# A hybrid decoder step on one core: loads, transposes and page loads of the S5 stage in another order

## The chip, the cores and the metric

The kernel runs on one NeuronCore of one Trainium2 chip. The metric is the device time of one execution in microseconds (us). The time before is the median of three runs.

## What is computed

One inference step of a small decoder: 256 prompt tokens and 8 sample tokens pass through one S5 layer (a complex diagonal state-space mixer) with its MLP and one sparse-attention layer with its MLP. The change touches the first stage of the program, in which two independent things are computed. One is the S5 mixer up to its gelu:

```python
bbar_r = zoh_r[..., None] * br - zoh_i[..., None] * bi
bu_r = jnp.einsum('btgc,gpc->btgp', u, bbar_r)
acr, aci, bcr, bci = lax.associative_scan(_complex_affine_combine, (a_r, a_i, bu_r, bu_i), axis=1)
sr = bcr + acr * s0r - aci * s0i
y = einsum(c_re, sr) - einsum(c_im, si)
z = jax.nn.gelu(y + d_skip * h) @ w_glu
```

The other depends on no token of this step: the compression of the paged cache, which the attention layer needs much later.

```python
past_cmp = cache_cmp_kv[page_table].reshape((nb, past_len) + row_shape)
blk = rows.reshape(nb, n_blk, CMP_BLOCK, 2, N_KV_HEADS, HEAD_DIM) + cmp_pos
hid = jax.nn.gelu(jnp.einsum('bnlsgd,sldh->bnsgh', blk, w1))
```

## The kernel before, in words

Activations lie feature by token: 8 tiles of 128 features by 264 tokens (`NT`). After the first stage come the gated projection `glu` (16 weight tiles), an MLP (64 weight tiles), keys and values, attention, the output projection and a second MLP. A weight tile is 512 KB; ACT splits it into a rounded part `wh` (L609), DVE into the rest `wl` (L610), and TensorE (PE) does three products of each part (L616 to L618). Four tiles of the pool `wr` hold raw weights, and the compression's weights `w` share these four.

The first stage, `s5_stage`, is written in the order in which it is to be issued (`manual_schedule`), and each engine takes its instructions in that order. Its steps, for the two halves h = 0 and 1 of the state slots:

- DVE makes the powers of the transition (`PT`, up to L270) and `e` (L325 to L328); ACT turns the last powers into `pr`, `pq`, `CQ` (`as_mult(PT, 3, 5, True)`, L257 to L306); DVE makes `E[h]` from them (`powers_in`, L332 to L335).
- PE sums the squares of the tokens (L309), DVE makes the norm's `rB` (L496 to L137) and scales the tokens `U` (L503); PE broadcasts `rB` (L510).
- `transpose_in(h)`: PE transposes `E[h]` (L349, 16 each), ACT copies it out (L351). `chunk_in(h)`: PE multiplies it with the tokens (L367, 64 each), ACT copies into the states `St`.
- DVE: `xhat` (L524), the powers on the output side `Fc[0]`, `Fc[1]` (`powers_out`, L383 to L386), the scan over chunks (`up` and `carry`, L443 to L446, then `down`, L465 and L466: slots 0 to 15, 16 to 23, 24 to 31). `Fc[0]` takes the buffer that `E[1]` leaves.
- PE: the convolution kernels (`kernels(h)`, L409 to L413), the convolutions (`conv`, L473) of eight feature tiles `ft`, and `from_states(ft)` (L482), which needs the scanned states of the tile's four slots. ACT: the gelu `ge` (L485, two buffers) and its rounded copy `gh` (L486). DVE: the rest `gl = ge - gh` (`rests`, L548), which frees `ge`.

Between these steps `filler(n)` advances the generator `sample_compress` by n pieces. For each of s = 0 (keys) and 1 (values) it runs 32 matmuls of 272 columns (L809; one instruction of the order is two matmul records of the trace), four groups `lc` of 8, two pieces a group. A page block `blk` has one buffer: 16 pages, one DMA each at a page number read from the table (128 KB, L788), and the position row (L789). So the block of s = 1 is loaded when the last matmul of s = 0 has read the block of s = 0. The counts are in a table:

```python
F = dict(m=2, n=4, o=3, q=4, r=5)
    K.load_cst()
    filler(1)
    as_mult(PT, 3, 5, True)
...
    filler(F["m"])
    gain(0)
    powers_in(0)
```

m stands ahead of `powers_in(0)`, n behind `chunk_in(0)`, o ahead of `powers_out`, q between `kernels(0)` and `kernels(1)`, r behind the first six convolutions. `load_cst` (L1501) and the two loads of `comp_loads` (L733, L736) are issued by ACT; all other loads of the stage but four early ones by the sync engine SP. SP reads the 16 page numbers by `value_load` with bounds (L781): a load from SBUF, an operation on the register and an assertion each. At the end of the stage DVE does:

```python
    for s0, n, late in ((0, 16, ()), (16, 8, (0, 1, 2, 3)), (24, 8, (4, 5))):
        down(s0, n)
        rests(late)
```

A transfer's completion is counted on one of eight semaphores (DMAHW0 to DMAHW7 in the order below). They go round, and a transfer waits, in its issuer's queue, for the earlier one on its semaphore.

Of the kernel before, what the change touches and what calls it, by code (L numbers as in the profile page):

```python
# [153 lines left out]

F = dict(m=2, n=4, o=3, q=4, r=5)


def s5_stage(K, filler):
# [141 lines left out]
    for h in range(2):  # L300
        S.activation(sq[:, h], U[:, h], AF.Square)
    K.load_cst()
    filler(1)
    as_mult(PT, 3, 5, True)
# [132 lines left out]
    def step(dst, src, n, i):  # L437

        sh = [128, 2, 32, n]
        a = tp.tile([128, 2, 32, 8], F32, tag="va", name="ca", bufs=1)[:, :, :, 0:n]  # L440
        b_ = tp.tile([128, 2, 32, 8], F32, tag="vb", name="cb", bufs=1)[:, :, :, 0:n]
        x, o = St[:, :, :, src:src + n], St[:, :, :, dst:dst + n]
        TT(a, x, SX[:, i, 1:2].to_broadcast([128, 2, 32]).unsqueeze(3).to_broadcast(sh), ALU.mult)  # L443
        TT(b_, x[:, ::-1], SX[:, i, 0:3:2].unsqueeze(3).to_broadcast(sh), ALU.mult)
        TT(o, o, a, ALU.add)
        TT(o, o, b_, ALU.add)  # L446
# [42 lines left out]

    filler(F["m"])  # L490
    gain(0)
# [54 lines left out]
    def rests(fts):  # L546
        for ft in fts:
            TT(yl[0][:, ft], ges[ft], yh[0][:, ft].bitcast(F32), ALU.subtract)  # L548
    for s0, n, late in ((0, 16, ()), (16, 8, (0, 1, 2, 3)), (24, 8, (4, 5))):
        down(s0, n)  # L550
        rests(late)
        for ft in range(s0 // 4, (s0 + n) // 4):
            ges[ft] = from_states(ft, pys[ft])
            if ft in (1, 3):
                expand(1, 4 * ft - 4, 8)
    K.last_scan = [i for i in nc.cur_bb.bb.instructions if i.engine == nc.vector.engine][-1]
    rests((6, 7))
# [171 lines left out]
def comp_loads(K):  # L729
    nc = K.nc  # L730
    c = K.cp
    K.w2 = c.tile([128, 4, 64], F32, name="w2")
    nc.scalar.dma_start(K.w2, K.A["cmp_w2"].rearrange("(x p) e -> p x e", p=128))  # L733

    K.gk = c.tile([128, 4, 64], F32, name="gk")
    nc.scalar.dma_start(K.gk.rearrange("p a d -> p (a d)"), K.A["gains"].broadcast_to((128, 256)))  # L736

# [39 lines left out]
def sample_compress(K):  # L777

    nc = K.nc
    S, V, G = nc.scalar, nc.vector, nc.gpsimd  # L780
    K.pages = [nc.sync.value_load(K.ptab[0:1, i:i + 1], min_val=0, max_val=NPOOL - 1) for i in range(16)]  # L781
    w1v = K.A["cmp_w1"]

    def load(s):
        blk = K.fil.tile([128, 17, 16, 16], F32, tag="blk", name="blk")
        f = lambda t: t.rearrange("p l x -> p (l x)")
        for pg in range(16):
            nc.sync.dma_start(f(blk[:, pg]), K.A["cache_cmp"][s, bass.ds(K.pages[pg], 1)].rearrange("o p x -> (o p) x"))  # L788
        nc.sync.dma_start(f(blk[:, 16]), K.A["cmp_pos"][s])  # L789
        return blk  # L790
# [5 lines left out]
    w = {(0, lc): load_w(0, lc) for lc in range(2)}  # L796
    blk = load(0)
    yield
    for lc in (2, 3):
        w[0, lc] = load_w(0, lc)  # L800
    comp_loads(K)
    yield
    for s in range(2):
        pts = [K.ps("fl"), K.ps("fl")]
        for lc in range(4):
            for l in range(4):
                for hf in range(2):
                    ll = 4 * lc + l
                    nc.tensor.matmul(pts[hf][:, 0:272], w[s, lc][:, l, 128 * hf:128 * hf + 128], blk[:, :, ll],  # L809
                                     start=(ll == 0), stop=(ll == 15))  # L810
                if l == 1:
                    yield
            if s == 0:
                w[1, lc] = load_w(1, lc)
            if s == 0 and lc == 3:
                blk = load(1)
            yield
        if s == 0:
            comp_setup(K)
# [648 lines left out]
def build(ctx, tc, A, O):  # L1468
# [31 lines left out]
    K.wr = ctx.enter_context(tc.tile_pool(name="wr", bufs=4))  # L1500
    K.load_cst = lambda: nc.scalar.dma_start(ctile, A["cst"])  # L1501

# [184 lines left out]
def inputs_of(x):  # L1687

    cat = np.concatenate
    cmp = x["cache_cmp_kv"].reshape(20, 4, 2, 8, 2, 2, 4, 64).transpose(5, 0, 4, 7, 2, 3, 1, 6).reshape(2, 20, 128, 256)  # L1690
    pos = x["cmp_pos"].reshape(2, 16, 128).transpose(0, 2, 1)
    slc, win = x["cache_slc_kv"], x["cache_win_kv"]
# [73 lines left out]
```

## Time and profile before

| | before |
|---|---|
| median of 3 runs | 757.06 us (756.28 to 759.0) |
| profiled execution, own time | 756.5 us |
| its span, first to last instruction | 754.7 us |
| mean granted TensorE clock | 0.948 |
| busy, share of the span | PE 94%, DVE 70%, ACT 54%, POOL 8% |
| DMA | 124.67 MB, mean 165 GB/s |

Times of rows are microseconds from the span's start. PE, PEld (weight loads), DVE, ACT, POOL are engines, SPq and ACTq the sequencers that issue DMAs; L12 is a line of the kernel. Text in brackets at the end of a row is the idle time of the engine just before it and what ended it. A wait for several things is put down to the one that came last.

### The profile page before, as it was taken

What the parts mean: (1) busy time and instruction counts of PE and PEld (TensorE: products, weight loads), DVE (VectorE), ACT (ScalarE), POOL (GpSimd) and SP (SyncE); (2) the same over time, 40 slices, a digit from 0 to 9 for tenths busy, and PEclk for the clock granted to TensorE, in tenths of its full rate; (3) what the DMA queues carried; (4) which work ended last, traced back from release to release, by engine and by line L of the source; (5) the groups of instructions that cost most, each with busy time, mean ns of one, the idle gap of its engine ahead of it and who ended that gap; (6) DMA issues with size and microseconds to landing.
All of it is one profiled execution on the core that took longest, in us unless ns stands there. A gap on an engine that the chain in (4) does not pass through costs nothing.

```text
span 754.7 us, 16057 instructions
## 1 busy us (share of the span) xinstructions
PE 709.4 (94%) x6160; PEld 644.4 (85%) x6160; DVE 525.7 (70%) x1154; ACT 404.9 (54%) x918; POOL 58.3 (8%) x103
## 2 busy tenths in 40 slices
PE   3495989999999999999989999999999999999998
PEld 1384879999999999999978956455799999999997
DVE  7679977988767756655776787746387777755553
ACT  4257246656666645444574666434376666644442
POOL 0100000210400000001022231100020000000000
PEclk9697999999999999999999968667999999999999
DMA  6714115665997655555546551000155555566651
GB/s 254 257 63 147 58 57 163 210 203 184 334 377 266 217 186 178 186 179 184 181 146 217 181 184 57 1 1 1 56 167 170 188 176 187 177 194 192 196 189 43
DMA packets 48430, 124.67 MB, mean 165 GB/s; under 512 B 5978, under 2 KB 21978, under 8 KB 48098
## 3 DMA queue, kind: packets, MB, share of 16 engines
q1 hardware_dynamic: 46818, 121.23, 48.8%
q10 hardware_dynamic: 1536, 2.42, 0.9%
q8 instruction: 48, 0.79, 0.4%
q14 instruction: 28, 0.23, 0.1%
HBM read 120.63 MB, written 7.18 MB: 169 GB/s over the span
## 4 chain that ended last, share of the span: by engine, by line
PE 87%; DVE 3%; SPq 3%; DMA 3%; ACT 2%; issue 2%; ACTq 0%; DVEq 0%
PE ps_mm L616 22%; PE ps_mm L617 21%; PE ps_mm L618 21%; PE ps_fl L809 5%; PE ps_sc L1213 3%; PE ps_tr L1250 2%; SPq L788 2%; PE ps_po L1271 2%; DMA raw<-w_up_in 1%; SPq L781 1%; PE ps_mm L1424 1%; PE ps_sc L1216 1%; DVE wl L610 1%; DMA xp<-x_cols_in 1%; PE ps_sc L1209 1%
## 5 line engine op out<-in xcount | busy, mean ns | idle before, releaser
L610 DVE TENSOR_TENSOR wl<-raw,wh 128x512 fp32r<-128x512 f32 x344 | 241.0, 705 | 145.4 <-ACT wh L609 143.1
L609 ACT ACTIVATE wh<-raw 128x512 fp32r<-128x512 f32 x344 | 215.3, 630 | 208.2 <-PE ps_mm L617 150.9
L616 PE MATMUL ps_mm<-hh,wh 128*128 128x264 f32 x512 | 145.2, 284 | 0.0
L617 PE MATMUL ps_mm<-hl,wh 128*128 128x264 f32 x512 | 145.0, 283 | 0.0
L618 PE MATMUL ps_mm<-hh,wl 128*128 128x264 f32 x512 | 145.0, 283 | 0.0
L617 PEld LDWEIGHTS ps_mm<-hl,wh 128*128 128x128 f32 x512 | 96.5, 188 | 0.0
L616 PEld LDWEIGHTS ps_mm<-hh,wh 128*128 128x128 f32 x512 | 96.4, 188 | 0.0
L618 PEld LDWEIGHTS ps_mm<-hh,wl 128*128 128x128 f32 x512 | 96.0, 187 | 0.0
L616 PE MATMUL ps_mm<-xhxl,wh 128*128 128x264 f32 x256 | 72.9, 285 | 0.0
L617 PE MATMUL ps_mm<-yl,wh 128*128 128x264 f32 x256 | 72.9, 285 | 0.0
L617 PE MATMUL ps_mm<-xhxl,wh 128*128 128x264 f32 x256 | 72.8, 285 | 0.0
L616 PE MATMUL ps_mm<-yh,wh 128*128 128x264 f32 x256 | 72.6, 284 | 0.0
L618 PE MATMUL ps_mm<-xhxl,wl 128*128 128x264 f32 x256 | 72.4, 284 | 0.2 <-DVE wl L610 0.2
L618 PE MATMUL ps_mm<-yh,wl 128*128 128x264 f32 x256 | 72.6, 284 | 0.0
L809 PE MATMUL ps_fl<-blk,w 128*128 128x272 f32 x128 | 35.6, 443 | 17.1 <-DMA xp<-x_cols_in 10.4
L618 PEld LDWEIGHTS ps_mm<-xhxl,wl 128*128 128x128 f32 x256 | 48.0, 188 | 0.4 <-DVE wl L610 0.4
L616 PEld LDWEIGHTS ps_mm<-xhxl,wh 128*128 128x128 f32 x256 | 48.2, 188 | 0.1
L616 PEld LDWEIGHTS ps_mm<-yh,wh 128*128 128x128 f32 x256 | 48.2, 188 | 0.0
L618 PEld LDWEIGHTS ps_mm<-yh,wl 128*128 128x128 f32 x256 | 48.2, 188 | 0.0
L617 PEld LDWEIGHTS ps_mm<-xhxl,wh 128*128 128x128 f32 x256 | 48.1, 188 | 0.0
L617 PEld LDWEIGHTS ps_mm<-yl,wh 128*128 128x128 f32 x256 | 48.1, 188 | 0.0
L809 PEld LDWEIGHTS ps_fl<-blk,w 128*128 128x128 f32 x128 | 27.3, 217 | 24.0 <-issue 10.8
(438 smaller groups left out, 1452.3 us busy)
## 6 DMA issues: line engine op xcount, KB each, us to landing
raw<-w_up_in SPq DMA_DIRECT2D x64, 512.0 KB, 4.3
raw<-w_down_in SPq DMA_DIRECT2D x64, 512.0 KB, 3.6
raw<-s_w_glu_in SPq DMA_DIRECT2D x16, 512.0 KB, 4.3
w<-cmp_w_in SPq DMA_DIRECT2D x12, 512.0 KB, 3.5
raw<-w_kv_in SPq DMA_DIRECT2D x12, 512.0 KB, 3.7
blk<-cache_cmp_in SPq DMA_DIRECT2D x32, 128.0 KB, 3.2
raw<-w_q_in SPq DMA_DIRECT2D x8, 512.0 KB, 4.1
win_old_out<-cache_win_kv_in SPq DMA_DIRECT2D x8, 510.0 KB, 6.3
```

Of the source, the lines that this page charges most:

```text
L609: nc.scalar.activation(h[:, :, cols], src[:, c:c + 4], AF.Copy)
L610: nc.vector.tensor_tensor(l[:, :, cols], src[:, c:c + 4], h[:, :, cols].bitcast(F32), ALU.subtract)
L616: nc.tensor.matmul(out, wh, xh, start=start, stop=False)
L617: nc.tensor.matmul(out, wh, xl, start=False, stop=False)
L618: nc.tensor.matmul(out, wl, xh, start=False, stop=stop)
L781: K.pages = [nc.sync.value_load(K.ptab[0:1, i:i + 1], min_val=0, max_val=NPOOL - 1) for i in range(16)]
L788: nc.sync.dma_start(f(blk[:, pg]), K.A["cache_cmp"][s, bass.ds(K.pages[pg], 1)].rearrange("o p x -> (o p) x"))
L809: nc.tensor.matmul(pts[hf][:, 0:272], w[s, lc][:, l, 128 * hf:128 * hf + 128], blk[:, :, ll], start=(ll == 0), stop=(ll == 15))
L1209: nc.tensor.matmul(banks[g2][:, 256 * r2:256 * r2 + 256], K.QT[hs[g2], 4 * gp + 2 * rp + r2, 0:128], K.KTp[hs[g2], gp, :, 0:128], start=Fa ...
L1213: nc.tensor.matmul(banks[g2], K.QT[hs[g2], 4 * gp + 2 * rp + u - 1, 128:256], K.KTp[hs[g2], gp], start=True, stop=False)
L1250: nc.tensor.transpose(pt[:, 128 * j:128 * j + 128], Pf[:, 128 * j:128 * j + 128], K.ident)
L1271: nc.tensor.matmul(po[64 * g2:64 * g2 + 64, 128 * kt:256], K.Vp[:, kt, br, 64 * g:64 * g + 64], rhs, start=False, stop=(br == 1 and kt == 1))
```

## The change

1. `load_cst` and the two loads of `comp_loads` are issued by SP, and `load_cst` stands earlier in the text.
2. The count m is gone, n keeps 4 and o becomes 5: no compression stands ahead of `powers_in(0)` and `transpose_in(0)`. Two pieces of the generator that only load are taken right behind the load of `xp`.
3. The block of pages is cut into halves of 8 rows each: 64 KB for a page, three buffers instead of one, 34 more DMAs. The tensors in HBM are laid out accordingly.
4. Page numbers are read without bounds.
5. The scan's products `ca` and `cb` lie in one `big` buffer of the pool instead of two small ones.
6. The rests of tiles 2 and 3 stand behind the last `down`, and the point behind which `glu` may be issued (`last_scan`) is that `down`.

```diff
-F = dict(m=2, n=4, o=3, q=4, r=5)
+F = dict(n=4, o=5, q=4, r=5)
     filler(1)
     xp = K.xp = e8([128, 8, NT], "xp")
     nc.sync.dma_start(xp, A["x_cols"])
+    filler(1)
+    K.load_cst()
+    filler(1)
...
-    K.load_cst()
-    filler(1)
     as_mult(PT, 3, 5, True)
...
-        a = tp.tile([128, 2, 32, 8], F32, tag="va", name="ca", bufs=1)[:, :, :, 0:n]
-        b_ = tp.tile([128, 2, 32, 8], F32, tag="vb", name="cb", bufs=1)[:, :, :, 0:n]
+        w = tp.tile([128, 2048], F32, tag="big", name="big")
+        a, b_ = (w[:, 512 * i:512 * i + 512].rearrange(...)[:, :, :, 0:n] for i in range(2))
...
-    filler(F["m"])
     gain(0)
...
-    for s0, n, late in ((0, 16, ()), (16, 8, (0, 1, 2, 3)), (24, 8, (4, 5))):
+    for s0, n, late in ((0, 16, ()), (16, 8, (0, 1)), (24, 8, (2, 3, 4, 5))):
         down(s0, n)
+        if s0 == 24:
+            K.last_scan = [i for i in nc.cur_bb.bb.instructions if i.engine == nc.vector.engine][-1]
         rests(late)
...
-    nc.scalar.dma_start(K.w2, ...)
+    nc.sync.dma_start(K.w2, ...)
-    nc.scalar.dma_start(K.gk.rearrange("p a d -> p (a d)"), ...)
+    nc.sync.dma_start(K.gk.rearrange("p a d -> p (a d)"), ...)
...
-    K.pages = [nc.sync.value_load(K.ptab[0:1, i:i + 1], min_val=0, max_val=NPOOL - 1) for i in range(16)]
+    K.pages = [nc.sync.value_load(K.ptab[0:1, i:i + 1]) for i in range(16)]
-    def load(s):
-        blk = K.fil.tile([128, 17, 16, 16], F32, tag="blk", name="blk")
+    def load(s, hf):
+        blk = K.fil.tile([128, 17, 8, 16], F32, tag="blk", name="blk", bufs=3)
...
-    blk = load(0)
+    blk = {(0, 0): load(0, 0)}
     yield
+    blk[0, 1] = load(0, 1)
     for lc in (2, 3):
         w[0, lc] = load_w(0, lc)
+    yield
     comp_loads(K)
+    blk[1, 0] = load(1, 0)
     yield
...
-            if s == 0 and lc == 3:
-                blk = load(1)
+            if s == 0 and lc == 1:
+                blk[1, 1] = load(1, 1)
...
-    K.load_cst = lambda: nc.scalar.dma_start(ctile, A["cst"])
+    K.load_cst = lambda: nc.sync.dma_start(ctile, A["cst"])
```

ACT's queue at the start of the stage, before (`sq`: squares of the tokens, `cst`, `w_389`, `gk`: the three late loads, `pr`, `pq`: the powers for `E`):

```order
L301 ACTIVATE sq<-U 128x1168 [waits DMAHW5_49]
L301 ACTIVATE sq<-U 128x1168 [waits DMAHW6_49]
L1501 DMA cst<-cst_in 128x1141 [waits DMAHW5_49]
L733 DMA w_389<-cmp_w_in 128x4x64 [waits DMAHW7_49]
L736 DMA gk<-gains_in 128x256 [waits DMAHW1_49]
L257 ACTIVATE pr<-px 128x128 [waits DVE_49]
L258 ACTIVATE pq<-px 128x4x16
```

and now:

```order
L304 ACTIVATE sq<-U 128x1168 [waits DMAHW5_49]
L304 ACTIVATE sq<-U 128x1168 [waits DMAHW6_49]
L260 ACTIVATE pr<-px 128x128 [waits DVE_49]
L261 ACTIVATE pq<-px 128x4x16
L262 ACTIVATE pq<-px 128x4x16
L307 ACTIVATE CQ<-pq 128x192 [waits Activation_49]
L330 ACTIVATE E_332<-e_333 128x32x16 [waits DVE_49]
```

The three DMAs with their waits have left ACT's queue; `pr` waits for DVE alone.

PE's queue at the same place, before (`sq,vec`: the sum of squares, `blk,w_261`: the first compression group, `ident,E_420`: the transposes of `E[0]`, `rB,vec`: the norm's broadcast):

```order
L309 MATMUL ps_tr<-sq,vec 128x511 x4
L309 MATMUL ps_tr<-sq,vec 128x292
L809 MATMUL ps_fl<-blk,w_261 128x272 x8
L349 MATMUL ps_tr<-ident,E_420 128x128 x16
L510 MATMUL ps_tr<-rB,vec 128x56
```

and now:

```order
L310 MATMUL ps_tr<-sq,vec 128x511 x4
L310 MATMUL ps_tr<-sq,vec 128x292
L350 MATMUL ps_tr<-ident,E_332 128x128 x16
L510 MATMUL ps_tr<-rB,vec 128x56
L510 MATMUL ps_tr<-rB,vec 128x7
```

The first group of the compression is gone from there. Behind `chunk_in(0)` two groups still stand ahead of the transposes of `E[1]`, as before, and two groups instead of one stand between `chunk_in(1)` and `kernels(0)`.

DVE's queue at the end of the stage, from the last two instructions of the last `down` on, before (`gl`: rests, `wl`: rests of the first weight tiles of `glu`, `z`: its first result):

```order
L465 TENSOR_TENSOR big<-St,sx 128x392
L466 TENSOR_TENSOR St<-St,big 128x8x7x7
L548 TENSOR_TENSOR gl<-ge,gh 128x264 x2
L610 TENSOR_TENSOR wl<-raw,wh 128x512 x4
L548 TENSOR_TENSOR gl<-ge,gh 128x264 x2
L610 TENSOR_TENSOR wl<-raw,wh 128x512 x3
L674 TENSOR_TENSOR z<-ps_mm,sg 128x264
```

and now:

```order
L466 TENSOR_TENSOR big<-St,sx 128x392
L467 TENSOR_TENSOR St<-St,big 128x8x7x7
L548 TENSOR_TENSOR gl<-ge,gh 128x264
L611 TENSOR_TENSOR wl<-raw,wh 128x512 x4
L548 TENSOR_TENSOR gl<-ge,gh 128x264 x5
L611 TENSOR_TENSOR wl<-raw,wh 128x512 x3
L675 TENSOR_TENSOR z<-ps_mm,sg 128x264
```

Of the four rests that stood ahead of the last `down`, two have moved behind it, and one of the later ones now stands ahead of the first weight tiles instead of two.

## Rows read from the trace of the kernel before

**Rows 1.** The page: busy us, share of the span and instructions of each engine.

```profile
PE 709.4 (94%) x6160; PEld 644.4 (85%) x6160; DVE 525.7 (70%) x1154; ACT 404.9 (54%) x918; POOL 58.3 (8%) x103
```

**Rows 2.** Waits, 0 to 125 us: engine, line <- releaser: us, times, longest.

```profile
ACT pr L257 <- DMA blk<-cache_cmp_in: 13.5, 1, 13.5
...
PE ps_fl L809 <- DMA blk<-cmp_pos_in: 6.7, 1, 6.7
```

**Rows 3.** Timeline, ACT's wait and DVE's: start, us, engine, line, operation.

```profile
15.89 0.69 DVE L328 TENSOR_TENSOR e<-e,big 128x512 f32<-128x512 f32 x1
...
22.24 0.36 ACTq L1501 DMA_DIRECT2D cst<-cst_in  x1
...
25.04 0.31 ACT L257 ACTIVATE pr<-px 128x128 f32<-128x128 f32 x1 [13.52 <-DMA blk<-cache_cmp_in]
...
25.38 1.76 DVE L332 TENSOR_TENSOR E<-e,pr 128x1536 f32<-128x1536 f32 x1 [8.80 <-ACT pr L257]
```

**Rows 4.** Timeline, from the norm to `powers_out(0)`.

```profile
11.07 7.22 PE L309 MATMUL ps_tr<-sq,vec 128*128 128x511 f32 x10 [11.07 <-DMA vec<-vecs_in]
...
28.84 1.76 DVE L335 TENSOR_TENSOR E<-E,big 128x1536 f32<-128x1536 f32 x1
...
34.74 0.36 DVE L137 SCALAR_TENSOR_TENSOR rB<-rs,rs 128x73 f32<-128x73 f32 x1
...
45.35 2.35 DVE L524 TENSOR_TENSOR xhat<-xp,rb 128x2112 f32<-128x2112 f32 x1
...
51.63 2.29 DVE L383 TENSOR_TENSOR Fc<-Cl,pr 128x2048 f32<-128x2048 f32 x1 [3.92 <-ACT ET L351]
```

**Rows 5.** The chain that ended last, PE's pieces, 0 to 125 us: start, us.

```profile
28.65 6.70 PE ps_fl L809 x16
...
37.13 2.67 PE ps_tr L510 x24
...
42.22 7.53 PE ps_fl L809 x32
49.75 1.78 PE ps_tr L349 x16
...
70.67 9.85 PE ps_fl L809 x32
...
102.08 2.63 PE ps_fl L473 x16
...
116.43 1.95 PE ps_fl L482 x120
```

**Rows 6.** Windows: stretch, busy us of PE, PEld, DVE, ACT, POOL, granted clock, DMA.

```profile
28.00:32.00 4.00, 3.35 (x8) 2.57 (x9) 3.93 (x5) 0.00 (x0) 0.00 (x0) 0.50 0.98 366
```

**Rows 7.** Timeline of DVE, the scan's end and what follows.

```profile
99.69 0.98 DVE L466 TENSOR_TENSOR St<-St,big 128x784 f32<-128x784 f32 x1
...
104.90 0.57 DVE L466 TENSOR_TENSOR St<-St,big 128x392 f32<-128x392 f32 x1
...
111.26 0.43 DVE L548 TENSOR_TENSOR gl<-ge,gh 128x264 fp32r<-128x264 f32 x1 [0.30 <-ACT gh L486]
...
115.81 0.57 DVE L466 TENSOR_TENSOR St<-St,big 128x392 f32<-128x392 f32 x1
...
116.98 2.49 DVE L610 TENSOR_TENSOR wl<-raw,wh 128x512 fp32r<-128x512 f32 x4
```

**Rows 8.** SP: page numbers and page loads (durations in ns min/median/max).

```profile
L781 SPq TENSOR_LOAD <-ptab x16: 263/263/469, 3.3 to 12.0; - x16
...
13.59 8.59 SPq L788 DMA_DIRECT2D blk<-cache_cmp_in  x16
...
L788 SPq DMA_DIRECT2D blk<-cache_cmp_in x32: 332/333/1281, 13.6 to 67.1; - x32
```

**Rows 9.** Timeline, gelu on ACT and the first products of `glu` on PE.

```profile
117.50 0.39 ACT L485 ACTIVATE ge<-ps_fl 128x264 f32<-128x264 f32 x1 [2.53 <-PE ps_fl L482]
...
123.88 0.29 PE L617 MATMUL ps_mm<-gl,wh 128*128 128x264 f32 x1
```

More of the change, by code (lines that the diff above doesn't have):

```diff
@@ L439, in step @@
         sh = [128, 2, 32, n]
-        a = tp.tile([128, 2, 32, 8], F32, tag="va", name="ca", bufs=1)[:, :, :, 0:n]
-        b_ = tp.tile([128, 2, 32, 8], F32, tag="vb", name="cb", bufs=1)[:, :, :, 0:n]
+        w = tp.tile([128, 2048], F32, tag="big", name="big")
+        a, b_ = (w[:, 512 * i:512 * i + 512].rearrange("p (r s n) -> p r s n", r=2, n=8)[:, :, :, 0:n] for i in range(2))
         x, o = St[:, :, :, src:src + n], St[:, :, :, dst:dst + n]
@@ L555, in s5_stage @@
                 expand(1, 4 * ft - 4, 8)
-    K.last_scan = [i for i in nc.cur_bb.bb.instructions if i.engine == nc.vector.engine][-1]
     rests((6, 7))
@@ L732, in comp_loads @@
     K.w2 = c.tile([128, 4, 64], F32, name="w2")
-    nc.scalar.dma_start(K.w2, K.A["cmp_w2"].rearrange("(x p) e -> p x e", p=128))
+    nc.sync.dma_start(K.w2, K.A["cmp_w2"].rearrange("(x p) e -> p x e", p=128))
     K.gk = c.tile([128, 4, 64], F32, name="gk")
-    nc.scalar.dma_start(K.gk.rearrange("p a d -> p (a d)"), K.A["gains"].broadcast_to((128, 256)))
+    nc.sync.dma_start(K.gk.rearrange("p a d -> p (a d)"), K.A["gains"].broadcast_to((128, 256)))
 def comp_setup(K):
@@ L780, in sample_compress @@
     S, V, G = nc.scalar, nc.vector, nc.gpsimd
-    K.pages = [nc.sync.value_load(K.ptab[0:1, i:i + 1], min_val=0, max_val=NPOOL - 1) for i in range(16)]
+    K.pages = [nc.sync.value_load(K.ptab[0:1, i:i + 1]) for i in range(16)]
     w1v = K.A["cmp_w1"]
-    def load(s):
-        blk = K.fil.tile([128, 17, 16, 16], F32, tag="blk", name="blk")
+    def load(s, hf):
+        blk = K.fil.tile([128, 17, 8, 16], F32, tag="blk", name="blk", bufs=3)
         f = lambda t: t.rearrange("p l x -> p (l x)")
         for pg in range(16):
-            nc.sync.dma_start(f(blk[:, pg]), K.A["cache_cmp"][s, bass.ds(K.pages[pg], 1)].rearrange("o p x -> (o p) x"))
-        nc.sync.dma_start(f(blk[:, 16]), K.A["cmp_pos"][s])
+            nc.sync.dma_start(f(blk[:, pg]), K.A["cache_cmp"][s, hf, bass.ds(K.pages[pg], 1)].rearrange("o p x -> (o p) x"))
+        nc.sync.dma_start(f(blk[:, 16]), K.A["cmp_pos"][s, hf])
         return blk
@@ L808, in sample_compress @@
                     ll = 4 * lc + l
-                    nc.tensor.matmul(pts[hf][:, 0:272], w[s, lc][:, l, 128 * hf:128 * hf + 128], blk[:, :, ll],
+                    nc.tensor.matmul(pts[hf][:, 0:272], w[s, lc][:, l, 128 * hf:128 * hf + 128], blk[s, lc // 2][:, :, ll % 8],
                                      start=(ll == 0), stop=(ll == 15))
@@ L1689, in inputs_of @@
     cat = np.concatenate
-    cmp = x["cache_cmp_kv"].reshape(20, 4, 2, 8, 2, 2, 4, 64).transpose(5, 0, 4, 7, 2, 3, 1, 6).reshape(2, 20, 128, 256)
-    pos = x["cmp_pos"].reshape(2, 16, 128).transpose(0, 2, 1)
+    cmp = x["cache_cmp_kv"].reshape(20, 4, 2, 8, 2, 2, 4, 64).transpose(5, 2, 0, 4, 7, 3, 1, 6).reshape(2, 2, 20, 128, 128)
+    pos = x["cmp_pos"].reshape(2, 2, 8, 128).transpose(0, 1, 3, 2)
     slc, win = x["cache_slc_kv"], x["cache_win_kv"]
@@ L1726, in inputs_of @@
         w_kv=tiles(x["w_kv"])[:, 0], w_q=wq, w_gate=w_in[:, 1024:1072].reshape(8, 128, 48).transpose(1, 0, 2), nsa_w_o=wo,
-        cmp_pos=np.repeat(pos[..., None], 16, -1).reshape(2, 128, 256),
+        cmp_pos=np.repeat(pos[..., None], 16, -1).reshape(2, 2, 128, 128),
         cmp_w1=x["cmp_w1"].reshape(2, 16, 128, 256).transpose(0, 2, 1, 3),
```

## The prediction, as put on record

> **What bounds the kernel now.** I began with the page: PE is busy 94% of the span, DVE 70% [rows 1]. That is an average. From about 118 us on PE streams products with small gaps, so the rest of the program moves with the moment at which `glu` can start, and nothing in the change edits what comes after. Only the first stage decides. There the waits name two large ones on engines that others wait for: ACT stands 13.5 us before `pr`, PE 6.7 us before a page block [rows 2].
>
> The timeline shows who pays for the first. DVE has finished `e` at 15.89 + 0.69 = 16.58 and sits idle until 25.38, 8.80 us, for `pr`; ACT starts `pr` at 25.04, right behind the DMA issues that began with `cst` at 22.24 [rows 3]. `pr` itself needs only DVE's powers, done before `e`. It is late because it is queued behind three DMAs which each wait for an older transfer on their semaphore (the order of ACT above), here page loads still in flight.
>
> Behind that, DVE runs without a gap to the end of `xhat` at 47.70, then waits 3.92 us for the buffer of `E[1]`, which PE's transposes leave at 51.63 [rows 4]. PE was late there: two compression groups, 7.53 us, stand ahead of the transposes [rows 5]. From 51.63 DVE has work without a gap to 104.90 + 0.57 = 105.47. Then the four rests ahead of the last `down` wait for gelus, and it ends only at 115.81 + 0.57 = 116.38 [rows 7]. PE brought the last convolutions at 104.71 [rows 5], so these gelus came late. So the stage is a chain DVE, PE, DVE, PE with three holes: 8.8, 3.9 and about 6 us.
>
> **Late loads on SP.** ACT reaches `pr` as soon as DVE's powers are there, before DVE needs it. `E` then starts at 16.58: 8.80 us earlier. The two ends are 8.80, where SP takes the waits, and 0, the second rival. I take 8.80: the row names a DMA as releaser and the DMA is no longer in ACT's queue.
>
> The row says that ACT's queue was blocked for 13.5 us [rows 2]. The Trainium skill (DMA: Bandwidth & Descriptors, Issuing engines are not separate DMA queues) says that all issuers share the same DMA engines and that spreading issues over several saves only the short time of issuing. By that, leaving ACT frees only three issues of about 0.36 us, 1.1 us in place of 8.8.
>
> On SP the three are issued behind the first two page halves. What waits behind them is the third half, needed by PE only near 57 us, so they cost nothing there.
>
> **Transposes ahead of the compression.** `E[0]` is ready at 28.84 + 1.76 = 30.60, now 21.80; `rB` at 35.10, now 26.30 [rows 4]. The sum of squares on PE ends at 18.3 [rows 4], so it is in time. The first compression group no longer blocks PE from 28.65 to 35.35 [rows 5], and the transposes fit between 21.8 and 26.3. From the broadcast to the start of the two groups behind `chunk_in(0)` PE took 42.22 - 37.13 = 5.1 us, the groups 7.53, and `Fc[0]` started 1.88 behind the transposes' start [rows 4, 5]. So `Fc[0]` starts at 26.3 + 5.1 + 7.5 + 1.9 = 40.8 if PE runs at its full clock. It will not quite: PE will have idled since 18.3, and the first group of before ran at a granted clock of 0.50, 1.2 GHz of 2.4 [rows 6], taking 6.70 us where half of 7.53 is 3.8: 2.9 us more [rows 5]. The ends are 0 and 2.9. I take 1.1, nearer to 0, because transposes and broadcast now run ahead of the compression and take some of the slow time in short instructions: 41.9. Below 38.9 it cannot go, since `xhat` ends there. Against 51.63 that is 9.7 us.
>
> **Three halves, three buffers.** The group moved behind `chunk_in(1)` makes PE's way to the last convolution longer by half of 7.53, 3.8 us. Its old way from the transposes' end (51.53) to that convolution (104.71) is 53.2 us [rows 5]. The 6.7 us for pages [rows 2] go, since the third half has a buffer of its own and is loaded early, and so do the 2.3 us by which the two groups behind that wait were slower than 7.53 (9.85, [rows 5]). 53.2 - 6.7 - 2.3 + 3.8 = 48.0, so PE is ready at about 89.8. DVE finishes the first `down` 49.0 us behind the start of `Fc[0]` (99.69 + 0.98 - 51.63, [rows 4, 7]), at 90.9. PE is 1 us ahead, and the first two rests have 3 us more, since they stand behind the second `down`. The cover is thin: if it goes, the first rival begins.
>
> SP pays for the halves: page issues come every 8.59/16 = 0.54 us [rows 8], so 34 more take 18 us. They start earlier, since the range checks go: one number took 0.56 us from load to load, of which the load is 0.26 [rows 8], so 16 save 4 to 5 us and the first half is issued by about 18 us and landed by 22. PE asks for it at 31. The second is issued by 28 and needed at 44, the third by 39 and needed at 57. The fourth follows the freed buffer at about 39, ends near 49 and is needed near 78. The weights `w` follow the freed buffers as before. So the checks alone bring nothing, and the halves cost nothing in the sum; the cover is at least 9 us everywhere.
>
> Of the page loads the rows show one every 0.54 us [rows 8]. The Trainium skill (DMA: Bandwidth & Descriptors, Rules for kernel authors) advises to coalesce small transfers, as under 64 KB one pays mostly overhead; a half page is just 64 KB. By that rule the halves speak against the change, which is the third rival.
>
> **One `big` buffer** for the scan's products: the order shows the same waits on DVE alone. Nothing.
>
> **The end.** From `Fc[0]` DVE needs 53.84 us to the second `down`'s end, two rests of 0.43, and 4.7 us for the last `down` (from about 111.7 to 116.38) [rows 4, 7]: 59.4 us, so it ends at 101.3 in place of 116.38, 15.1 us earlier. Something is given back. Rests 3 to 7 now stand behind four `wl` of `glu`, 2.49 us [rows 7], and a gelu waits until the rest of two tiles before has freed its buffer. Counted from the last `down`'s end: rest 2 and the `wl` 2.9, rest 3 by 3.35, then three times gelu (0.39) and copy (0.42), 5.8, and the last rest 6.25 [rows 7, 9]. The first two tiles of `glu` are 48 products, about 0.12 us apart; some 22 remain then, 2.7 us, so they are done at about 9.0. Before they were done at 124.0, 7.6 behind [rows 9]. That gives back 1.4. The bounds are 0 and 3.5 (all of the waiting added to the rate of before).
>
> **The sum.** 15.1 - 1.4 = 13.7 us. From the profiled execution's 756.5 (span 754.7 and 1.8 around it) that is 742.8; the median of the runs is 0.56 higher, so **743.4 us**. Everything behind moves as one, since its loads follow buffers that PE frees.
>
> **Rivals.**
>
> 1. *PE becomes the bound.* The compression's clock stays low longer, or drops in a short idle stretch, in two or more groups behind the transposes: 2.9 us each [rows 5], less about 3 of cover. For: the 1 us of cover, and the low clock seen before at such starts [rows 6]. Against: with the page wait gone PE has no long idle stretch. Two groups give 746.3, four 752. Chance 0.12.
> 2. *ACT's wait is not the queue.* `E` starts at 25.38 as before. PE would still do the transposes at once, `rB` stays at 35.10, `Fc[0]` starts at 35.1 + 5.1 + 7.5 + 1.9 = 49.6, 2.0 earlier, and the end gives 64.75 - 59.4 - 1.4 = 3.9: 751.2 us. For: a wait is put down to what came last. Against: `pr` has only DVE in its waits now. By the skill's rule above on issuers the time would be near this. Chance 0.04.
> 3. *SP becomes the bound, slower than before.* If a half page takes the 1.28 us that one issue took at worst [rows 8] in place of 0.54, SP needs 4 x 20.9 us and some 12 for the rest: the last half lands near 99, the last groups end at 107, the convolutions at 110, from there to the last `down` 11.7 us passed before [rows 5, 7], and I estimate 9 with two rests fewer, so the stage ends near 119 + 1.4 against 116.4: about 761. It eats into the gain from 0.95 us a page on and loses from 1.25. For: twice as many transfers, half as long. Against: the median issue is 0.33 us [rows 8], with 128 KB. The skill's advice to coalesce would point here. Chance 0.04.
>
> **Chances and range.** Forecast 0.80. About 0.5% (3.8 us) is what a measurement of this kernel can tell from no change. Forecast, the second rival and nearly all of the first lie beyond it: faster 0.94; same 0.03 (the edges of the first and third); slower 0.03. The low end takes `Fc[0]` at 40.8 and nothing given back, 740.9, and a little for the spread of runs: 740.0. The high end takes 43.7 and 3.5 given back, 747.3, which holds the first case of rival 1, and the same spread: 748.5.
>
> **What would show it.** Right: ACT `pr` near 14 us and no DVE wait there; `Fc[0]` near 42 behind a DVE wait of 3 us; no PE wait for pages; last `down` ending near 101; rests 3 to 7 behind the `wl`. Wrong: DVE waiting at the first rests (rival 1), `E` near 25 (rival 2), L809 waiting for pages with SP issuing all the time (rival 3), or a stage that ends near 101 while the sum of the rest has grown.

## The result and the profile after

The changed kernel takes 746.13 us (median of 4 runs, 745.02 to 747.1) against 756.67 us, a ratio of 0.9857, 95% interval 0.9828 to 0.9886: faster by 10.5 us. The forecast was 743.4 with a range of 740.0 to 748.5. The profiled execution took 747.1, with a span of 745.3 and a mean granted clock of 0.956.

The page's busy times, beside [rows 1], show that nothing was saved in work; what went is idle time.

```profile
PE 708.7 (95%) x6160; PEld 645.8 (87%) x6160; DVE 526.0 (71%) x1154; ACT 404.5 (54%) x918; POOL 55.7 (7%) x103
```

The first half of the forecast came as written. The timeline of DVE (start, duration, engine, line, operation) answers to [rows 3, 4]:

```profile
16.75 1.76 DVE L333 TENSOR_TENSOR E<-e,pr 128x1536 f32<-128x1536 f32 x1
...
36.52 2.35 DVE L524 TENSOR_TENSOR xhat<-xp,rb 128x2112 f32<-128x2112 f32 x1
45.13 2.29 DVE L384 TENSOR_TENSOR Fc<-Cl,pr 128x2048 f32<-128x2048 f32 x1 [6.26 <-ACT ET L352]
```

`E` starts at 16.75 without a wait (16.58 was forecast), `xhat` ends at 38.87 (38.9). Then `Fc[0]` waits 6.26 us, twice the forecast, and starts at 45.13 in place of 41.9. ACT's own row shows that only DVE holds `pr` now:

```profile
14.02 0.31 ACT L260 ACTIVATE pr<-px 128x128 f32<-128x128 f32 x1 [3.02 <-DVE px L273]
```

PE's timeline between `E[0]` and the second transposes, beside [rows 5], shows where the 3.2 us went:

```profile
22.12 3.65 PE L350 MATMUL ps_tr<-ident,E 128*128 128x128 f32 x16 [5.16 <-DVE E L336]
26.47 5.25 PE L510 MATMUL ps_tr<-rB,vec 128*128 128x56 f32 x24 [0.70 <-ACT ET L352]
...
35.68 7.57 PE L813 MATMUL ps_fl<-blk,w 128*128 128x272 f32 x32
43.09 1.95 PE L350 MATMUL ps_tr<-ident,E 128*128 128x128 f32 x16
```

The order is the wanted one and PE has no wait behind 26.47, but the broadcast takes 5.25 us where [rows 5] has 2.67, and the first transposes 3.65 where the second take 1.95. The windows (busy us of PE, PEld, DVE, ACT, POOL, granted clock, DMA share, GB/s) give the reason, the lower of the two clocks, 1.2 GHz, on a PE that is busy all the time from 27 us on:

```profile
20.00:22.00 2.00, 0.00 (x0) 0.00 (x0) 1.97 (x3) 0.00 (x0) 0.00 (x0) 0.80 0.80 169
22.00:27.00 5.00, 4.18 (x19) 3.84 (x19) 4.55 (x15) 2.39 (x4) 0.00 (x0) 0.50 0.82 287
27.00:32.00 5.00, 5.00 (x25) 5.00 (x24) 4.93 (x6) 0.00 (x0) 0.00 (x0) 0.50 0.43 122
32.00:34.00 2.00, 2.00 (x65) 1.98 (x69) 1.97 (x2) 1.04 (x4) 0.00 (x0) 0.50 0.90 286
34.00:36.00 2.00, 1.96 (x78) 1.80 (x71) 2.00 (x2) 1.77 (x7) 0.00 (x0) 0.79 0.97 328
36.00:44.00 8.00, 8.00 (x41) 6.74 (x40) 2.83 (x4) 1.80 (x8) 1.04 (x4) 1.00 0.64 191
```

The end of the stage, beside [rows 7], is the forecast one. DVE's timeline:

```profile
98.95 0.77 DVE L548 TENSOR_TENSOR gl<-ge,gh 128x264 fp32r<-128x264 f32 x2
...
103.84 0.57 DVE L467 TENSOR_TENSOR St<-St,big 128x392 f32<-128x392 f32 x1
104.33 0.43 DVE L548 TENSOR_TENSOR gl<-ge,gh 128x264 fp32r<-128x264 f32 x1
104.67 2.49 DVE L611 TENSOR_TENSOR wl<-raw,wh 128x512 fp32r<-128x512 f32 x4
...
109.95 0.43 DVE L548 TENSOR_TENSOR gl<-ge,gh 128x264 fp32r<-128x264 f32 x1 [0.30 <-ACT gh L487]
```

The first two rests no longer wait, and the last `down` ends at 103.84 + 0.57 = 104.41, 59.28 us behind the start of `Fc[0]` (forecast: 59.4). The first sigmoid of `glu`, the first thing that needs all of this stage, comes 10.56 us earlier. Its row of before, then that of the changed kernel:

```profile
123.72 0.39 ACT L672 ACTIVATE sg<-ps_mm 128x264 f32<-128x264 f32 x1
```

```profile
113.16 0.39 ACT L673 ACTIVATE sg<-ps_mm 128x264 f32<-128x264 f32 x1
```

From the last `down` to it there were 123.72 - 116.38 = 7.34 us, and now 113.16 - 104.41 = 8.75: 1.41 are given back, where 1.4 was forecast. From it to the span's end there were 631.0 us, now 632.1. So the whole gain is made ahead of the sigmoid, and the miss there, 3.2 us, is the start of `Fc[0]`. Of the 4.3 us between the forecast of the profiled execution, 742.8, and its 747.1, the other 1.1 lie behind the sigmoid.

One thing is needed to read the experiments: single executions of one kernel differ by up to 20 us (738.80 to 758.74 for the kernel before), and the profiled ones differ most in the granted clock between 425 and 530 us, far behind the edits, so parts are compared at the first sigmoid, and a median only says where both together ended.

### The profile page after: what moved, and what is told of

It is laid out like the page before. It is cut to its first block, busy times and chain, and to the rows that moved or that the text cites. A ratio compares the mean times of both kernels' runs of the same rounds, so it can differ in the third digit from the quotient of the medians.

```text
span 745.3 us, 16132 instructions
## 1 busy us (share of the span) xinstructions
PE 708.7 (95%) x6160; PEld 645.8 (87%) x6160; DVE 526.0 (71%) x1154; ACT 404.5 (54%) x918; POOL 55.7 (7%) x103
## 4 chain that ended last, share of the span: by engine, by line
PE 81%; DVE 10%; DMA 4%; SPq 2%; issue 1%; ACT 1%; DVEq 0%; ACTq 0%
PE ps_mm L618 22%; PE ps_mm L617 22%; PE ps_mm L619 22%; PE ps_sc L1217 3%; PE ps_tr L1254 2%; PE ps_po L1275 2%; DMA w<-cmp_w_in 1%; DMA raw<-w_up_in 1%; DVE big L466 1%; DVE St L467 1%; PE ps_fl L813 1%; PE ps_mm L1428 1%; SPq L789 1%; PE ps_sc L1220 1%; DVE St L447 1%
## 5 line engine op out<-in xcount | busy, mean ns | idle before, releaser
L648 POOL TENSOR_TENSOR nacc<-nacc,sq 128x264 f32<-128x264 f32 x21 | 17.7, 844 | 322.1 <-ACT sq L647 241.4
L1236 ACT ACTIVATE P<-ps_sc,nm 128x128 f32<-128x128 f32 (+1 forms) x64 | 26.3, 427 | 26.9 <-DVE nm L1234 20.2
```

What stands on the lines that cost most here:

```text
L648: nc.gpsimd.tensor_tensor(self.acc, self.acc, sq, ALU.add)
L1236: S.activation(P[:, i], sv[:, i], AF.Exp, bias=nm[:, i:i + 1], accum_out=den[:, i:i + 1])
```

## Experiments

All runs, from their profiled executions (us from the span's start; "behind" is from the sigmoid to the span's end):

| | `E` | `Fc[0]` | last `down` ends | sigmoid | behind | median of all runs |
|---|---|---|---|---|---|---|
| before | 25.38 | 51.63 | 116.38 | 123.72 | 631.0 | 756.67 |
| changed | 16.75 | 45.13 | 104.41 | 113.16 | 632.1 | 746.13 |
| changed, again | 16.70 | 44.24 | 103.53 | 112.28 | 630.3 | 744.33 |
| loads back on ACT | 23.97 | 53.72 | 112.95 | 121.72 | 623.8 | 744.54 |
| before, loads on SP | 17.44 | 49.97 | 114.57 | 123.47 | 615.7 | 753.33 |
| compression first | 17.92 | 45.36 | 104.57 | 113.32 | 623.5 | 738.60 |
| whole blocks | 17.34 | 43.35 | 107.98 | 117.11 | 629.6 | 750.58 |
| rests as before | 16.62 | 46.40 | 108.39 | 117.76 | 623.9 | 744.42 |
| range checks | 16.74 | 46.43 | 105.69 | 114.43 | 627.6 | 742.87 |
| PE kept busy | 17.69 | 46.84 | 106.09 | 114.84 | 617.5 | 737.51 |
| PE dense twice | 17.32 | 43.56 | 102.82 | 111.57 | 629.4 | 743.44 |
| groups behind transposes | 16.62 | 39.67 | 101.79 | 111.85 | 625.1 | 739.12 |
| both | 17.05 | 39.08 | 99.84 | 110.26 | 630.2 | 740.03 |
| one first, two late | 16.64 | 38.68 | 99.15 | 107.89 | 625.9 | 735.16 |

Where nothing behind `Fc[0]` is edited, the sigmoid follows it by 68.0 us (113.16 - 45.13, 112.28 - 44.24, 121.72 - 53.72, 113.32 - 45.36, 114.43 - 46.43). The column `Fc[0]` and a departure from 68.0 are the two things to read. `Fc[0]` itself lies between 43.35 and 46.43 in the five executions that have the changed kernel's order on PE and its early `E` (changed, changed again, whole blocks, rests, range checks), so a difference of 1 to 2 us there decides nothing.

**The changed kernel again.** No edit.

> The changed kernel once more, unedited, beside the other three, since in the runs so far the part behind glu's first sigmoid took between 616 and 632 us in the profiled executions, with stretches at a granted clock of 0.50 between 430 and 525 us that some executions have and others don't, whatever was edited in the first stage. Theory (that part has its own variation): the first sigmoid at 113.2 to 114.5 again, and single times spread over 740 to 748. Rival (the variation belongs to the edits): the first sigmoid as before and all times within 745 to 747.1.

Single times 740.35 to 746.76, the sigmoid at 112.28. The late part does vary by itself, so the rival falls as it stands; and `Fc[0]` of the same code moved by 0.9 us, since the low clock lay elsewhere (rows in the section on the hardware). That the edits have no part in it isn't shown: in four edited kernels (compression first, PE kept busy, groups behind transposes, one first) all 23 executions took less than 740 us, and none of the ten of the changed kernel did. Only the last of them has a sigmoid so much earlier that it would explain this; for the other three the cause stays open.

**Part 1 undone.**

```diff
-    K.load_cst = lambda: nc.sync.dma_start(ctile, A["cst"])
+    K.load_cst = lambda: nc.scalar.dma_start(ctile, A["cst"])
...
-    nc.sync.dma_start(K.w2, ...)
+    nc.scalar.dma_start(K.w2, ...)
-    nc.sync.dma_start(K.gk.rearrange("p a d -> p (a d)"), ...)
+    nc.scalar.dma_start(K.gk.rearrange("p a d -> p (a d)"), ...)
...
         S.activation(sq[:, h], U[:, h], AF.Square)
+    K.load_cst()
+    comp_loads(K)
```

Their two other calls are taken out.

> The changed kernel with cst, w2 and gk issued by ACT again, between the squares and pr. Theory (an issue that waits for its semaphore blocks all of ACT behind it): pr starts late again, between 18 and 25 us, E and everything up to Fc[0] by as much later than 16.6, and the time is 749 to 755. Rival (ACT's queue costs only the issues themselves, 0.36 us each in the kernel before): pr is 1.1 us later, below DVE's own time for e (16.6), and the time stays at 746.

ACT's timeline of this run:

```profile
18.64 0.37 ACTq L1505 DMA_DIRECT2D cst<-cst_in  x1
19.52 0.42 ACTq L735 DMA_DIRECT2D w<-cmp_w_in  x1
23.23 0.35 ACTq L738 DMA_DIRECT2D gk<-gains_in  x1
23.63 0.31 ACT L259 ACTIVATE pr<-px 128x128 f32<-128x128 f32 x1 [11.24 <-DMA w<-cmp_w_in]
```

The queue blocks ACT for 11 us though its three issues take 1.1 together; `pr` is 9.6 us late, `E` 7.2 and the sigmoid 8.6 (9.4 against the second unedited execution). The 1.4 between `E` and the sigmoid are within what that stretch varies by. The theory holds on the stage; its total does not show it, since the part behind ran 8 us shorter here.

**Part 1 alone, in the kernel before.**

```diff
-    K.load_cst = lambda: nc.scalar.dma_start(ctile, A["cst"])
+    K.load_cst = lambda: nc.sync.dma_start(ctile, A["cst"])
-    nc.scalar.dma_start(K.w2, ...)
+    nc.sync.dma_start(K.w2, ...)
-    nc.scalar.dma_start(K.gk.rearrange("p a d -> p (a d)"), ...)
+    nc.sync.dma_start(K.gk.rearrange("p a d -> p (a d)"), ...)
```

> The kernel before with only cst, w2 and gk moved to SP. Theory (two holes in series on two engines, of which PE's ends later): pr at 14 and E at 16.6 us as in the changed kernel, 8.8 us earlier, rB near 26.3; but PE still starts its first group when the pages are there, near 28.7, at a clock of 0.50, and has no idle time from there to the transposes of E[1], so Fc[0] stays near 51.6 and the time within 1 us of the kernel before, 756. Rival (ACT's wait is worth what it is long): 748.

`E` comes at 17.44, 7.94 us earlier, but `Fc[0]` only at 49.97, 1.66 earlier, and the sigmoid at 123.47, 0.25 before the kernel before. PE's timeline has two waits, ahead of the first group and ahead of the groups of s = 1:

```profile
26.79 6.91 PE L809 MATMUL ps_fl<-blk,w 128*128 128x272 f32 x16 [9.13 <-DMA blk<-cmp_pos_in]
...
68.50 10.20 PE L809 MATMUL ps_fl<-blk,w 128*128 128x272 f32 x32 [6.23 <-ACT Bb L340]
```

The first group still waits until its block has landed, at 26.79 in place of 28.65, and runs at 0.50 as before; so 6.3 of the 7.9 us are lost ahead of `Fc[0]`. The second wait is about as long as the 6.7 us of [rows 2]. The last `down` is still 1.81 earlier. The rest goes at the end of the stage, where PE's granted clock was 0.84 from 113.5 to 124.5 us (1.00 from 115 to 125 in the kernel before). On the stage the theory holds: needed, and alone worth little. The times, 740.27 to 756.4, spread over 16 us and decide nothing.

**The order on PE undone.**

```diff
-F = dict(n=4, o=5, q=4, r=5)
+F = dict(m=2, n=4, o=3, q=4, r=5)
...
+    filler(F["m"])
     gain(0)
```

> The changed kernel with the order on PE of the kernel before: one compression group ahead of the first transposes, two behind chunk_in(0), one behind chunk_in(1). Theory (low clock): the first group runs from 22 to 24 us on, when its half page has landed, at a clock of 0.50 in about 6.7 us, as in the kernel before; behind it transposes, broadcast and chunk_in run at 1.00, and two groups follow: 29 to 31 + 1.9 + 5.1 + 7.5 + 1.9 puts Fc[0] at 45.5 to 47.5, and the time at 746 to 748.5, so this part is worth 0 to 2 us. Rival (the forecast's own sum, with transposes at full clock): the order is worth about 4 to 5 us, 750.5.

`Fc[0]` at 45.36 and the sigmoid at 113.32, with `E` 1.2 us later than in the changed kernel: the new order shows no gain on the stage. PE's timeline shows the trade: the group costs 5.59 us in a hole, and transposes and broadcast behind it run at full clock. The clock falls later, in `chunk_in` (0.50 from 33 to 36 us), so the two groups start at 35.49.

```profile
21.89 5.59 PE L814 MATMUL ps_fl<-blk,w 128*128 128x272 f32 x16 [4.28 <-DMA blk<-cmp_pos_in]
27.32 1.94 PE L350 MATMUL ps_tr<-ident,E 128*128 128x128 f32 x16
29.10 2.83 PE L511 MATMUL ps_tr<-rB,vec 128*128 128x56 f32 x24
```

The median, 738.60, is below that of the changed kernel, by a part behind the sigmoid that took 623.5 us.

**Whole blocks.** One buffer of 16 rows a page, loaded again behind group 4 (`bufs=3` and the index `hf` taken out, the tensors in HBM as before).

> The changed kernel with whole page blocks in one buffer, as in the kernel before; the order on PE, the loads on SP and the missing checks stay. Theory: the first block is in time (needed at 35.7), but the second waits until the fourth group has freed the buffer (54.8 us); 17 issues at 0.54 us and the landing bring it to about 65, where PE asks at 59.9: PE waits 4 to 6 us, the last convolutions end near 97 and not 91.7, behind DVE's first down (94.2), so 1 to 4 us reach glu: its first sigmoid at 114.5 to 117. Rival (PE's cover takes all of it): 113.2 to 114.5.

PE's timeline shows the wait:

```profile
65.75 9.98 PE L811 MATMUL ps_fl<-blk,w 128*128 128x272 f32 x32 [7.48 <-DMA blk<-cmp_pos_in]
```

The sigmoid follows `Fc[0]` by 73.8 in place of 68.0 us: the halves are worth 5.7. The sigmoid itself, at 117.11, is 4.0 later than in the changed kernel, at the theory's upper end, since `Fc[0]` happened to come at 43.35. The theory had the wait at 4 to 6 (it was 7.48) and no slow matmuls behind it (32 records in 9.98 us, where 32 take 7.57 at full clock), so the last convolutions ended at 99.94 and not near 97.

**Rests as before.**

```diff
-    for s0, n, late in ((0, 16, ()), (16, 8, (0, 1)), (24, 8, (2, 3, 4, 5))):
+    for s0, n, late in ((0, 16, ()), (16, 8, (0, 1, 2, 3)), (24, 8, (4, 5))):
```

`last_scan` is set behind the loop again.

> The changed kernel with the end of the stage as in the kernel before: rests 0 to 3 behind the second down, 4 and 5 behind the last, and glu's wl behind them. Theory: rests 2 and 3 need gelus that come after the first two have freed their buffers, so DVE stands some 4 us ahead of the last down, which ends near 108.4 in place of 104.4; glu then follows in 7.6 us as in the kernel before and not in 9.0, so about 2.6 us are lost: 748.7. Rival: what glu starts by is the last gelu, which does not care: 746.

71.4 us from `Fc[0]` to the sigmoid, 3.3 more than in the changed kernel (2.6 was expected). DVE waits 1.60 and 0.30 us ahead of the last `down`, and takes two rests more there; the last `down` ends 61.99 us behind `Fc[0]` in place of 59.28:

```profile
102.54 0.43 DVE L548 TENSOR_TENSOR gl<-ge,gh 128x264 fp32r<-128x264 f32 x1 [1.60 <-ACT gh L487]
103.28 0.43 DVE L548 TENSOR_TENSOR gl<-ge,gh 128x264 fp32r<-128x264 f32 x1 [0.30 <-ACT gh L487]
```

From there to the sigmoid it takes 9.37 us, not the 7.6 of the theory. PE was at the low clock there, as this window shows; in the kernel before and in the changed one it was not.

```profile
108.00:112.00 4.00, 3.56 (x121) 3.39 (x121) 3.83 (x8) 0.81 (x2) 0.00 (x0) 0.50 0.20 35
```

With the 7.34 us of the kernel before in place of 9.37, an estimate, this part would be worth 1.3. So it is worth between 1.3 and 3.3 us; whether the order brings the low clock about is not shown.

**Range checks back.** `min_val=0, max_val=NPOOL - 1` in `value_load`.

> The changed kernel with the range checks on the page numbers again. Theory: SP reaches its first load of w some 4 us later (12.6 and not 8.6 us); the first half page is needed at 35.7 and had landed by about 24, so nothing changes: 746 within 1 us. Rival: SP's later issues delay xp (26.2 us) and the loads behind it, and the second half page or w come after PE asks: up to 4 us, 750.

`E` and the norm are as before the edit (16.74), and SP's first `w` goes out at 12.30 and not 8.59, but no wait for pages appears on PE. `Fc[0]` is 1.3 us later because the clock stayed at 0.50 until about 37.8 us, in place of 34.8 (8.38 us for the groups, against 7.57). 68.0 us follow. No cost of the checks is shown.

**PE kept busy.**

```diff
+    pd = ps("mm")
+    for i in range(6):
+        nc.tensor.matmul(pd[:, 0:511], sameT, sqf[:, 0:511], start=True, stop=True)
```

behind the sum of squares.

> The changed kernel with six products of 128x511 added on PE between the sum of squares (which ends at 17.0 us there) and the transposes (22.1 us); they go into a PSUM tile that nobody reads, so the output is the reference's. Theory (the low clock): the changed kernel's PE ran from 22 to 34.8 us at a granted clock of 0.50, and that alone put the two compression groups at 35.70 and Fc[0] at 45.13. With PE kept busy the clock should stand at 1.00 from 22 us on, the 16 transposes take 1.95 us as in the kernel before and not 3.65, the broadcast 2.8 and not 5.25, the groups start at 26.3 + 5.1 = 31.4, Fc[0] at 40.8 to 41.0, the last down ends near 100.2 and the time is about 742. Rival (the chain of waits read literally): the groups start when a transfer of w lands at 35.7; then Fc[0] stays at 45 and the time at 746, whatever the clock does.

Neither theory came out. The transposes ran fast (2.21 us), then PE waited 2.14 us for `rB`, the clock fell at 27.9 in the broadcast (4.96 us), and the groups started at 36.82. The median, 737.51, would have looked like the theory's success; the sigmoid, 1.7 us later than in the changed kernel with `E` 0.9 later, says that it isn't. So idle time ahead of the transposes is not the whole cause.

**PE dense twice.** Three such products more, between the transposes and the broadcast.

> The changed kernel with nine products of 128x511 into a PSUM tile that nobody reads: six between the sum of squares and the transposes (as in the run that kept PE busy) and three between the transposes of E[0] and the broadcast; the output is the reference's. With the first six alone the transposes ran at full clock, but the clock fell at 27.9 us, in the broadcast, behind a wait of 2.1 us for rB, and the two groups started at 36.8. Theory (the clock falls behind idle time): without that wait the clock holds, the broadcast takes 2.8 us and not 5, the groups start near 32.5 and Fc[0] near 42; glu's first sigmoid is near 110.5 (113.16 in the changed kernel). Rival (the many small products of chunk_in, 64x73, let it fall whatever stands ahead, as it fell at 33 us in the run with the compression first): the broadcast is fast, but the clock falls in chunk_in and the groups start at 34 to 36. Second rival (a transfer of w sets it): 35.7 and Fc[0] at 45 whatever the clock is.

PE's timeline, and the windows:

```profile
22.95 1.95 PE L353 MATMUL ps_tr<-ident,E 128*128 128x128 f32 x16
24.73 2.74 PE L510 MATMUL ps_mm<-sq,vec 128*128 128x511 f32 x6
27.31 2.73 PE L515 MATMUL ps_tr<-rB,vec 128*128 128x56 f32 x24
...
34.03 7.60 PE L818 MATMUL ps_fl<-blk,w 128*128 128x272 f32 x32
```

```profile
27.00:30.00 3.00, 3.00 (x27) 2.88 (x26) 2.96 (x4) 0.00 (x0) 0.00 (x0) 1.00 0.48 131
30.00:34.00 4.00, 4.00 (x131) 3.92 (x130) 3.93 (x4) 2.72 (x10) 0.00 (x0) 0.57 0.82 272
34.00:42.00 8.00, 8.00 (x45) 6.69 (x38) 5.40 (x5) 1.61 (x7) 1.81 (x4) 1.00 0.70 213
```

The first rival came out: with PE at work without a gap from 17.8 us on and full clock through the broadcast, the clock still falls among the 64x73 products of `chunk_in`, and the groups start at 34.03, 1.6 us later than at full clock (27.31 + 5.1 = 32.4). The second rival falls: the groups follow the clock, not a transfer. `Fc[0]` is at 43.56, within the spread of the kernel without these products, whose groups started at 33.96 in its second execution; so no gain of the products is shown.

**Groups behind the second transposes.** `filler(F["n"])` moved from behind `chunk_in(0)` to behind `transpose_in(1)`.

> The changed kernel with the two compression groups moved once more, from behind chunk_in(0) to behind transpose_in(1). Theory (DVE's 6.3 us wait before Fc[0] is those 7.55 us of PE): the second transposes start at about 35.7, end at 37.6, and Fc[0] starts at 38.9, where xhat ends, 6.2 us earlier. But PE's work up to the last convolutions is the same and PE has only some 2 us of cover there (it idles from about 92 to 94 us), so DVE then waits at the first two rests or in the second down, and about 2 us are left: 743.5 to 745. Rival (the cover is larger, since the rests stand behind the second down): all 6.2 us arrive, 740. Second rival (PE was the bound already): 746.

`Fc[0]` at 39.67, 5.5 us earlier, the sigmoid at 111.85, 1.3 earlier (0.4 against the second unedited execution): PE is the bound then, as the theory had it: its last convolutions end at 93.75, behind DVE's first `down` (91.61). DVE waits 2.75 us at `Fc[1]`, and less is left than the theory's 2 us. The median, 739.12, is again helped by the part behind.

**Both.** PE kept busy and the groups moved.

> Both edits together: the six products that keep PE busy, and the two groups behind transpose_in(1). If the low clock is what costs PE its 4.3 us, PE is ready at the last convolutions near 88 and not 92 us, Fc[0] starts at 38.9, the first down ends near 88, and the two gains add to about 6 us: 740. If the clock is not the cause, this run gives what the moved groups give alone (743.5 to 745).

The sigmoid at 110.26, 2.0 to 2.9 us before the unedited executions. Less than the 6 expected, since the last convolutions ended at 91.80 (91.71 in the changed kernel): PE was not ready earlier. The clock held through the broadcast and then fell (0.52 from 30 to 32 us), and PE waited 1.88 us for `rB` and 1.75 for `E[1]`.

**One first, two late.** The counts of the order undone, with the two groups behind `transpose_in(1)`: one group ahead of the first transposes, two behind the second, one behind `chunk_in(1)`.

> The changed kernel with one compression group ahead of the first transposes, as in the kernel before, and the two that stood behind chunk_in(0) behind transpose_in(1). Theory: the first group runs while PE would wait for E[0], and PE is ready at the last convolutions near 88 us, as in the run with the compression first (88.4), while DVE no longer waits for 7.5 us of PE before Fc[0], which starts near 39.7, as in the run with the groups behind the transposes. Both gains then add: the first down ends near 89, and glu's first sigmoid is at 107.5 to 110, 3 to 5.5 us before the changed kernel. Rival (PE stays the bound): 111.9, as with the moved groups alone.

DVE's timeline no longer has a wait at `Fc[0]`:

```profile
36.41 2.35 DVE L525 TENSOR_TENSOR xhat<-xp,rb 128x2112 f32<-128x2112 f32 x1
38.68 2.32 DVE L384 TENSOR_TENSOR Fc<-Cl,pr 128x2048 f32<-128x2048 f32 x1
```

The last convolutions end at 87.23, the sigmoid is at 107.89, 4.4 to 5.3 us before the unedited executions, as the theory had it. Part of it may be luck: the first group ran at full clock here (3.91 us, against 5.59 with the order undone). The median is 735.16 against 744.33 for the changed kernel and 756.14 for the kernel before, measured beside it; its times, 728.44 to 735.75, all lie below those of the changed kernel, 740.35 to 746.76. About half of the 9.2 us is this stage; the rest lies behind it and is not shown to be the edit's.

## Why the prediction was right, and where its size was off

- **Late loads on SP**: right, 8.6 us of `E` (8.80), and the queue is shown to be the cause. The Trainium skill (DMA: Bandwidth & Descriptors, Issuing engines are not separate DMA queues) counts only the issuing time, which is 1.1 us here; undoing this part cost 8.6 us at the sigmoid, so here the measurement decides against pricing the move by that alone: the waits in front of the issues were the price. The second rival falls.
- **Transposes ahead of the compression**: this is the step that failed. "The ends are 0 and 2.9. I take 1.1, nearer to 0, because transposes and broadcast now run ahead of the compression and take some of the slow time in short instructions." From the broadcast's start to the groups' PE took 9.21 us in place of 5.1, so this term was 4.1 and not 1.1, beyond its upper end. The upper end, 2.9, came from a compression group at the low clock [rows 5, 6], behind which the clock was back. Transposes, broadcast and most of `chunk_in` ran at 0.50, from 22 to about 34.8 us. In the five executions with this order `Fc[0]` lay at 43.35 to 46.43, and the same stretch took 6.85 to 9.72 us: the size of the term varies with the clock, but it was over 1.1 every time. With the order undone the stage ended at the same time: what the move won in order it lost in clock. Why the clock stayed low is open.
- **Halves**: right that the 6.7 us of page wait go and that SP is in time; undone, they cost 5.7. From the transposes' end to the last convolutions' PE took 46.7 us (45.04 to 91.71), 48.0 was forecast. The third rival, SP as the bound, falls: PE shows no wait for pages, though a half page took 0.56 to 0.70 us of issuing and not 0.54, and the fourth half was out at 56.9 and not 49 (needed at 81.2). PE was ready ahead of DVE's first `down` (it waited 2.32 us for it). So the first rival's low clock did come, but it delayed DVE and PE alike and did not make PE the bound.
- **The end**: 59.28 of 59.4 us, and 1.41 of 1.4 given back. Undoing the order of the rests costs 1.3 to 3.3 us.
- **Range checks**: no cost shown, as forecast.
- **The sum**: 13.7 - 3.2 (the start of `Fc[0]`) = 10.5, against 10.56 at the sigmoid. The parts undone one by one cost 8.6, 5.7 and 1.3 to 3.3, over 15 in all, more than the 10.6 they bring together, and the first alone brings 0.25: the holes lay in series on different engines, so closing one lets the next open. That the median came so close also rests on the part behind the sigmoid, which took 632.1 us in the profiled execution, near the 631.0 of before, and 615.7 to 630.3 in the other runs; that agreement is luck. At the sigmoid every term of the sum but the one came out within 0.2 us of the forecast.

## What to carry to other kernels

In this kernel a wait in front of a DMA issue held everything behind it on the issuing engine (13.5 and 11.2 us on ACT): look for compute instructions that a DMA releases though they read none of its data. Price a hole only together with what comes next on the other engine, by undoing one part at a time. Where matmuls are moved into a place behind idle time, let the upper bound take all of them at the low clock (here 9.2 us in place of 5.1), and look for work that is ready to stand in the gap ahead. A compression group there gave transposes and broadcast full clock in two runs, but not all of `chunk_in`. Compare variants at a mark behind the edited stage where a later stage varies by itself.

## What the runs showed of the hardware

A PE that is busy all the time can be at the low clock: 0.50 from 22 to about 34.8 us of the changed kernel, with transposes, the broadcast and 64x73 products, and without a gap from 26.5 us on. Among the same products the clock fell at full occupation in the run with PE dense twice, and, behind a compression group, in the run with the order undone. In the kernel before, also behind a compression group, they ran at 1.00, as this window shows:

```profile
35.00:42.00 7.00, 7.00 (x171) 6.77 (x170) 6.86 (x8) 3.97 (x12) 1.62 (x3) 1.00 0.23 77
```

The 64x73 products of `chunk_in(1)` in the changed kernel ran at 1.00 too (44 to 48 us). So neither the products nor what stood ahead of them settles it, and what does is not shown. When the clock falls and rises differs between executions of the same code. The second execution of the changed kernel had these windows where the first stood at 0.50 from 22 to 32 us:

```profile
20.00:24.00 4.00, 1.94 (x9) 1.97 (x10) 3.83 (x8) 0.60 (x1) 0.00 (x0) 0.75 0.84 273
24.00:27.00 3.00, 2.20 (x15) 1.93 (x13) 2.69 (x10) 1.79 (x3) 0.00 (x0) 0.77 0.79 232
27.00:32.00 5.00, 5.00 (x93) 4.98 (x97) 4.93 (x6) 1.27 (x4) 0.00 (x0) 0.68 0.52 140
```

The same happens on a larger scale in the attention stage. Windows of the kernel before, and of its variant with the loads on SP, whose first sigmoid came 0.25 us earlier and whose part behind it was 15.3 us shorter:

```profile
460.00:500.00 40.00, 38.28 (x183) 20.14 (x179) 26.68 (x83) 19.82 (x83) 5.22 (x14) 0.73 0.09 28
500.00:530.00 30.00, 30.00 (x199) 17.57 (x199) 17.80 (x59) 14.10 (x62) 0.00 (x0) 0.80 0.00 1
```

```profile
460.00:500.00 40.00, 37.53 (x265) 20.71 (x266) 33.41 (x106) 24.27 (x103) 4.56 (x10) 1.00 0.09 28
500.00:530.00 30.00, 30.00 (x238) 21.31 (x237) 17.11 (x48) 13.72 (x50) 0.00 (x0) 1.00 0.11 36
```

Whether an edit upstream makes the one or the other likelier stays open: the kernel before showed a time near 740 once (738.8) in 11 executions, the variant twice (740.27, 740.95) in 6.
